# All of layer 1's modulation and both MLP gates: from TensorE to sums on VectorE, GpSimd and ScalarE inside the MLPs

## The chip, the core and the metric

The kernel runs on one core of a Trainium2 chip. The metric is the device time of one execution in microseconds, the median of the runs shown. The engines are named as in the profile: PE is TensorE (PEld its weight loads), DVE is VectorE, ACT is ScalarE, POOL is GpSimd, SP is the engine that issues most DMAs.

## What is computed

One step of a two-layer transformer block on 384 tokens (128 context, 256 latent) of 1024 features. Each layer takes a modulation from a conditioning vector, one vector `m` for the context tokens and one for the latent tokens:

```python
e = silu(m) @ w_ada + b_ada                       # w_ada: 1024 x 6144, per layer
sh1, sc1, g1, sh2, sc2, g2 = split(e, 6)          # 1024 each
h = rmsnorm(x, g_mix) * (1 + sc1) + sh1
x = x + g1 * (mix(h) @ w_out)                     # mix: projection, four head groups
hf = rmsnorm(x, g_ffn) * (1 + sc2) + sh2
x = x + g2 * (square(relu(hf @ w_ff1)) @ w_ff2)   # 1024 -> 4096 -> 1024
```

`mix` is a projection into four groups (neighbourhood attention A, differential attention B, latent attention C, spatial gating D). So `sh1, sc1` are wanted when a layer begins, `g1, sh2, sc2` at its output projection, and `g2` only at the second matrix of its MLP. Everything is float32.

## The kernel before

Activations lie feature by token: a tile is 128 features by 384 tokens, and `x` is eight such tiles. Each large product is made of three float32r products (`mm3`, lines 201 to 203): weights and activations are split into a high part (a cast on ScalarE, L192) and a low part (raw minus high, L193, on VectorE or, where `pool` is set, on GpSimd). `load_split` first calls `load_raw` (L185), which issues a DMA of 512 KB on SP's queue into one of seven raw buffers; high and low parts have four buffers each.

An MLP runs in two halves. Each half makes 16 hidden tiles (24 matmuls each), then eight output tiles with two weight tiles each (48 matmuls). A hidden tile is read out of PSUM by VectorE (L1028, L1029), goes through relu and square on ScalarE (L1031, L1033), is squared in full on GpSimd (L1034), and VectorE takes the low part (L1035). An output tile is added to `x` with its gate by VectorE (`residual`, L852). In the second half of layer 0, `gained` (L363 to L364) and `sq_add` (L340) prepare layer 1's inputs from each output tile, and `load_layer(1)` fetches layer 1's small constants at output tile 0.

The modulation is made in three ways:
- `ada_quarter` (L293): layer 0's `sh1, sc1`, at the start, by TensorE.
- `ada(l, g)` (L228): a third of a layer's modulation (2048 columns) by TensorE, with silu(m) as the 32 stationary columns and raw weights streaming past; 16 raw tiles, 32 matmuls (64 records), then four transposes and an addition of the bias. `ada(l, 1)` gives `g1, sh2` and `ada(l, 2)` gives `sc2, g2`, in both layers. They are generators in a list `todo`, and `fill` advances the first by a step (two raw tiles) between the pieces of attention.
- `ada_rows` (L270): layer 1's `sh1, sc1`, by VectorE in layer 0's MLP. Weights are stored transposed (an output feature per partition), `silu_rows` makes silu of both vectors on every partition (it loads 1 MB into the tile that held the keys of group C), and one instruction multiplies 1024 weights by a vector and sums along the row. A block of 128 features takes one raw tile and two such sums; there are 16 blocks. The products that nobody needs go to a scratch `junk`, which has the one buffer of the small constants, and onto the raw tile.

The attention stage (`attend`) goes through units of a head and a block of tokens; after each it calls `pull`, for the next pieces of projections and output blocks, and `fill`. The fractions FILL_A, FILL_B, FILL_C say how many of both. The framework orders each engine's instructions by program order and expected readiness; an engine then executes in that order and waits at the first instruction that isn't ready. SP's queue is in order too.

Of the kernel before, what the change touches and what calls it, by code (L numbers as in the profile page):

```python
# [13 lines left out]
AF = mybir.ActivationFunctionType  # L14
# [66 lines left out]
def hybrid_step(ctx: ExitStack, tc: tile.TileContext, I, O):  # L81
# [15 lines left out]
    def sb(pool, shape, tag, bufs=None, dt=F32):  # L97
        return pool.tile(shape, dt, name=nm(tag), tag=tag, bufs=bufs)
# [41 lines left out]
    def V(n):  # L140
        a, b = VC[n]
        return vec[:, a:b]
# [105 lines left out]
        E[l, g] = eT  # L248


    def silu_rows():
        t = sb(act, [P, 2 * D], "kC", 1)
        nc.sync.dma_start(t, I["m_rows"])
        for c in range(0, 2 * D, 512):
            u = sb(wk, [P, 512], "pc", 3)
            nc.vector.tensor_scalar_max(u, t[:, c:c + 512], -40.0)
            nc.scalar.activation(u, u, AF.Exp, scale=-1.0)
            nc.scalar.activation(u, u, AF.Ln, bias=1.0)
            nc.scalar.activation(u, u, AF.Exp, scale=-1.0)
            nc.vector.tensor_mul(t[:, c:c + 512], t[:, c:c + 512], u)  # L260
        return t


    def ada_rows(rows, junk):
        eT = sb(lay, [P, 16, 2], "eT0")
        t = sb(lay, [P, 16, 2], "eTs")
        for b in range(16):
            raw = load_raw(I["w_adaT"][b], D)
            for v, out in enumerate((junk[:, 0:D], raw)):
                nc.vector.tensor_tensor_reduce(  # L270
                    out, raw, rows[:, v * D:(v + 1) * D], 1.0, 0.0, ALU.mult, ALU.add, t[:, b, v:v + 1]
                )
            yield
        nc.vector.tensor_add(
            eT, t, V("b_ada1")[:, 0:16].rearrange("p (j o) -> p j o", o=1).to_broadcast([P, 16, 2])
        )
        E[1, 0] = eT

# [285 lines left out]
    for l in range(L):  # L566
# [35 lines left out]
        else:  # L602

            for b in range(6):
# [2 lines left out]
                    mm3(accs[b][:, 0:TX], [t[:, k * P:(k + 1) * P] for t in w], hx1[k], k == 0, k == KD - 1)  # L607
                if b == 0:
                    rstd = x_rstd(acc)
        todo.append(ada(l, 1))  # L610
        todo.append(ada(l, 2))
        kfA = pair()
        nc.gpsimd.dma_start(kfA[:, :, 0:TP], I["kc"][l, 0])

# [391 lines left out]

        complete(work, last)
        e1 = M["e1"] = ada_done(l, 1)
        e2 = ada_done(l, 2)
        M["g2"] = gain(e2[:, 0:8, :], V(f"g_ffn{l}"))  # L1010
        for g in outs:
            for _ in g:
                pass
# [5 lines left out]
        for half in range(2):  # L1019
            hid = []  # L1020
            for m in range(KF // 2):
                w = load_split(I["w_ff1"][l, half * (KF // 2) + m], 1024)
                a = ps_mm()
                for k in range(KD):
                    mm3(a[:, 0:TX], [t[:, k * P:(k + 1) * P] for t in w], hs[k], k == 0, k == KD - 1)
                r = sb(wk, [P, TX], "rl", 2)[:, 0:T]
                bias = sb(wk, [P, 2], "rb", 2)
                nc.vector.tensor_copy(bias, a[:, T:TX])  # L1028
                nc.vector.tensor_mul(r, a[:, 0:T], rstd)  # L1029
                for v, (c, d) in enumerate(((0, TP), (TP, T))):  # L1030
                    nc.scalar.activation(r[:, c:d], r[:, c:d], AF.Relu, bias=bias[:, v:v + 1])  # L1031
                hi, lo = hilo()
                nc.scalar.activation(hi, r, AF.Square)  # L1033
                nc.gpsimd.tensor_mul(r, r, r)  # L1034
                nc.vector.tensor_sub(lo, r, hi.bitcast(F32))  # L1035
                hid.append((hi, lo))
                if l + 1 < L:
                    if half == 0 and m == 3:
                        rows = silu_rows()
                        junk = sb(lay, [P, SMW], "small", 1)  # L1040
                        todo.append(ada_rows(rows, junk))
                    fill(m % 3 == 2)
            for m in range(KD):
                a = ps_mm()
                for q in range(2):
                    w = load_split(I["w_ff2"][l, half, m, q], 1024, q)
                    for i in range(8):
                        k = 8 * q + i
                        mm3(a[:, 0:T], [t[:, i * P:(i + 1) * P] for t in w], hid[k], k == 0, k == 15)
                residual(a, m, e2[:, 8:16, :])  # L1050
                if half == 0:
                    fill()
                else:
                    if l + 1 < L:
                        if m == 0:
                            e0 = ada_done(1, 0)
                            load_layer(1)
                            g1 = gain(e0[:, 8:16, :], V(f"g_mix{l + 1}"))
                            hx1 = []
                        hx1.append(gained(m, g1[:, m, :], e0[:, m, :]))  # L1060
                    if m < KD - 1 or l + 1 < L:
                        sq_add(acc, m)
                    if l + 1 == L and m < 3:

                        if m % 2 == 0:
                            ys.append(pair())
                        nc.scalar.activation(
                            ys[m // 2][:, m % 2, :], x[:, m, :], AF.Copy, scale=V("g_final")[:, m:m + 1]
                        )
# [183 lines left out]
```

## Time and profile before

| | |
|---|---|
| median of 3 runs | 1021.88 us (1017.98 to 1025.13) |
| profiled execution | 1022.66 us, of which the profile's span is 1020.8 |
| mean granted clock of TensorE | 0.987 of 2.4 GHz |
| busy: PE, DVE, ACT, POOL | 966.7, 631.8, 461.6, 269.8 us |
| layer 0's MLP | about 248 to 521 us of the span |
| layer 1's projection and attention | about 521 to 738 |
| layer 1's MLP | about 738 to 1007 |

A row of the profile names the line, the engine, the operation and its tiles (output <- inputs); "idle before" is time in which that engine stood before the instruction, with what ended the wait.

### The profile page before, as it was taken

Reading aid. Unit: us, or ns where it says so; the run is one execution under the profiler, and the core shown is the slowest. Engines: PE = TensorE matmul, PEld = TensorE weight load, DVE = VectorE, ACT = ScalarE, POOL = GpSimd, SP = SyncE. Lnnn points to the kernel's source line nnn. Section 1 sums busy time; section 2 is a strip of 40 time slices with the busy share of each in tenths; the row PEclk is TensorE's granted clock in tenths of the full one; section 3 lists DMA queues with packets and bytes.
Section 4 is the critical chain, followed back from the end, with each engine's and each line's share of the span. In section 5 each row is a group of like instructions: output and inputs, shape, how many; then the busy total and the mean of one; then the engine's idle time right before and its main releaser. Section 6 shows DMA issues by size and latency. Waiting matters only on the chain.

```text
span 1020.8 us, 14701 instructions
## 1 busy us (share of the span) xinstructions
PE 966.7 (95%) x5358; PEld 852.1 (83%) x5358; DVE 631.8 (62%) x1285; ACT 461.6 (45%) x917; POOL 269.8 (26%) x240
## 2 busy tenths in 40 slices
PE   6999899898999999999998979998999999999995
PEld 2687566578998999999997756656999999999994
DVE  4475588879677556646676738886865322554453
ACT  3343576665553224553334427575455422455320
POOL 2353140220224211132243415111021421113221
PEclk9999899999999999999999998999999999999998
DMA  9868585735454555433435475663433334333301
GB/s 360 317 190 261 186 261 179 281 107 158 153 167 143 186 205 182 152 120 122 129 112 198 140 248 176 243 215 120 160 109 125 120 124 139 126 125 109 122 1 62
DMA packets 54744, 169.20 MB, mean 166 GB/s; under 512 B 7856, under 2 KB 11856, under 8 KB 54288
## 3 DMA queue, kind: packets, MB, share of 16 engines
q1 hardware_dynamic: 44928, 152.54, 43.7%
q0 software_dynamic: 6048, 10.94, 3.8%
q10 hardware_dynamic: 3696, 4.79, 1.5%
q8 instruction: 42, 0.69, 0.3%
q14 instruction: 30, 0.25, 0.1%
HBM read 160.19 MB, written 8.03 MB: 165 GB/s over the span
## 4 chain that ended last, share of the span: by engine, by line
PE 55%; DVE 5%; issue 2%; POOL 2%; DMA 2%; ACT 2%; ACTq 1%; DVEq 0%; POOLq 0%
PE mm L202 17%; PE mm L201 17%; PE mm L203 17%; PE ada L228 1%; DMA raw<-in_w_inT 1%; PE t L510 1%; ACT whi L192 1%; PE t L497 1%; DVE pair L198 1%; POOL h L349 1%; DMA pair<-in_bias 1%; ACTq L390 0%; DVE wlo L193 0%; POOL wlo L193 0%; DVE h L351 0%
## 5 line engine op out<-in xcount | busy, mean ns | idle before, releaser
L201 PE MATMUL mm<-pair,whi 128*128 128x384 f32 (+1 forms) x1296 | 443.9, 343 | 9.3 <-ACT pair L197 4.4
L202 PE MATMUL mm<-pair,whi 128*128 128x384 f32 (+1 forms) x1296 | 440.2, 340 | 5.0 <-DVE pair L198 3.7
L203 PE MATMUL mm<-pair,wlo 128*128 128x384 f32 (+1 forms) x1296 | 438.8, 339 | 0.0
L192 ACT CAST whi<-raw 128x1024 fp32r<-128x1024 f32 (+2 forms) x188 | 194.0, 1034 | 341.9 <-PE mm L202 262.8
L201 PEld LDWEIGHTS mm<-pair,whi 128*128 128x128 f32 x1296 | 243.0, 188 | 24.2 <-ACT pair L197 9.4
L202 PEld LDWEIGHTS mm<-pair,whi 128*128 128x128 f32 x1296 | 244.1, 188 | 9.7 <-DVE pair L198 7.0
L203 PEld LDWEIGHTS mm<-pair,wlo 128*128 128x128 f32 x1296 | 245.0, 189 | 3.4 <-issue 3.3
L193 DVE TENSOR_TENSOR wlo<-raw,whi 128x1024 fp32r<-128x1024 f32 (+2 forms) x135 | 162.7, 1205 | 88.9 <-ACT whi L192 88.3
L193 POOL TENSOR_TENSOR wlo<-raw,whi 128x1024 fp32r<-128x1024 f32 (+1 forms) x53 | 128.8, 2431 | 325.7 <-ACT whi L192 310.5
L1034 POOL TENSOR_TENSOR rl<-rl 128x384 f32<-128x384 f32 x64 | 58.3, 912 | 264.9 <-ACT pair L1033 150.8
L1035 DVE TENSOR_TENSOR pair<-rl,pair 128x384 fp32r<-128x384 f32 x64 | 40.1, 626 | 80.8 <-POOL rl L1034 80.8
L852 DVE SCALAR_TENSOR_TENSOR x<-mm,eT,x 128x128 f32<-128x128 f32 x96 | 35.5, 411 | 62.5 <-PE mm L203 62.5
L1031 ACT ACTIVATE rl<-rl,rb 128x128 f32<-128x128 f32 (+1 forms) x128 | 51.1, 446 | 21.1 <-DVE rl L1029 20.9
L228 PE MATMUL ada<-raw,sT 128*32 128x512 f32 x256 | 46.7, 606 | 0.0
L497 PEld LDWEIGHTS t<-ident,pl 128*128 128x128 f32 x144 | 17.0, 140 | 24.7 <-issue 15.4
L1029 DVE TENSOR_TENSOR rl<-mm,xr 128x384 f32<-128x384 f32 x64 | 35.0, 548 | 0.1
L1033 ACT ACTIVATE pair<-rl 128x384 fp32r<-128x384 f32 x64 | 33.6, 525 | 2.0
L480 ACT ACTIVATE pl<-s,nmx 128x384 f32<-128x384 f32 x48 | 28.0, 583 | 13.6 <-DVE nmx L476 13.2
L476 DVE TENSOR_REDUCE nmx<-s 128x1 f32<-128x384 f32 x48 | 26.3, 549 | 10.6 <-PE s L953 6.4
L270 DVE CUSTOM_DVE_ANT_0 small<-raw,kC 128x1024 f32<-128x1024 f32 x16 | 22.6, 1413 | 15.5 <-DMA raw<-in_w_adaT 15.5
L497 PE MATMUL t<-ident,pl 128*128 128x128 f32 x144 | 24.9, 279 | 5.9 <-DVE pl L997 4.5
L498 ACT COPY pair<-t 128x384 f32<-128x384 f32 x48 | 22.5, 478 | 15.9 <-PE t L497 10.2
(261 smaller groups left out, 1096.1 us busy)
## 6 DMA issues: line engine op xcount, KB each, us to landing
raw<-in_w_ff SPq DMA_DIRECT2D x128, 512.0 KB
raw<-in_w_ada SPq DMA_DIRECT2D x64, 512.0 KB
raw<-in_w_inT SPq DMA_DIRECT2D x20, 512.0 KB
adaq<-in_w_ada SPq DMA_DIRECT2D x32, 256.0 KB
raw<-in_w_out SPq DMA_DIRECT2D x16, 512.0 KB
raw<-in_w_adaT SPq DMA_DIRECT2D x16, 512.0 KB
raw<-in_w_inV SPq DMA_DIRECT2D x8, 512.0 KB
raw<-in_w_inV SPq DMA_DIRECT2D x8, 416.0 KB
```

Source lines behind the costliest of these rows:

```text
L192: nc.scalar.copy(hi, raw)
L193: (nc.gpsimd if pool else nc.vector).tensor_sub(lo, raw, hi.bitcast(F32))
L201: nc.tensor.matmul(out, lhsT=l[0], rhs=r[0], start=start, stop=False)
L202: nc.tensor.matmul(out, lhsT=l[0], rhs=r[1], start=False, stop=False)
L203: nc.tensor.matmul(out, lhsT=l[1], rhs=r[0], start=False, stop=stop)
L228: nc.tensor.matmul(acc[32 * j:32 * j + 32, :], lhsT=sT[:, k, :], rhs=raw[j // 2][:, (j % 2) * 512:(j % 2) * 512 + 512], start=(k == 0), st ...
L497: nc.tensor.transpose(tp[:, c * P:(c + 1) * P], p[:, c * P:(c + 1) * P], ident)
L852: nc.vector.scalar_tensor_tensor(x[:, m, a:b], acc_ps[:, a:b], gate[:, m, v:v + 1], x[:, m, a:b], ALU.mult, ALU.add)
L1029: nc.vector.tensor_mul(r, a[:, 0:T], rstd)
L1031: nc.scalar.activation(r[:, c:d], r[:, c:d], AF.Relu, bias=bias[:, v:v + 1])
L1034: nc.gpsimd.tensor_mul(r, r, r)
L1035: nc.vector.tensor_sub(lo, r, hi.bitcast(F32))
```

## The change

`ada` is kept for `ada(0, 1)` alone. A new `ada_half(0)` makes `sc2` of layer 0 in the old way from 1024 columns. All else goes through a class `Rows`, a list of blocks that are made one at a time by `step`: layer 0's `g2` (8 blocks) and all of layer 1's modulation but its `g2` gate (40 blocks) in layer 0's MLP, and layer 1's `g2` (8 blocks) in layer 1's MLP. A block goes to VectorE (two multiply-and-sum instructions, as before) or to GpSimd and ScalarE: GpSimd multiplies (`tensor_mul`, twice), ScalarE passes over the product and sums it. `silu_rows` is called at hidden tile 1 in both layers, and `load_layer(1)` moves from output tile 0 to output tile 7 of the second half.

```diff
+    def ada_half(l):
+        acc = ps_ada()
+        for kk in range(KD // 2):
+            raw = [load_raw(I["w_ada"][l, 2, 2 * kk + i, 0], 1024) for i in range(2)]
+            for i in range(2):
+                for h in range(2):
+                    j = 2 * i + h
+                    nc.tensor.matmul(
+                        acc[32 * j:32 * j + 32, :],
+                        lhsT=sT[:, 2 * kk + i, :],
+                        rhs=raw[i][:, h * 512:h * 512 + 512],
+                        start=(kk == 0), stop=(kk == KD // 2 - 1),
+                    )
+            yield
...
+    class Rows:
...
+        def begin(self):
+            self.rows = silu_rows()
+            self.junk = sb(lay, [P, SMW], "small", 1)
+
+        def add(self, l, name, first, n):
+
+            eT = sb(lay, [P, n, 2], f"eT{name}")
+            for b in range(n):
+                self.items.append((l, name, first, n, b, eT))
+
+        def step(self, vector=0, pool=0):
+            for i in range(vector + pool):
+                if not self.items:
+                    return
+                l, name, first, n, b, eT = self.items.pop(0)
+                raw = load_raw(I["w_adaT"][first + b + (8 if l else -40)], D)
+                for v in range(2):
+                    row = self.rows[:, v * D:(v + 1) * D]
+                    if i < vector:
+                        nc.vector.tensor_tensor_reduce(
+                            raw if v else self.junk[:, 0:D], raw, row, 1.0, 0.0, ALU.mult, ALU.add,
+                            eT[:, b, v:v + 1],
+                        )
+                    else:
+                        to = raw if v else self.junk[:, D:2 * D]
+                        nc.gpsimd.tensor_mul(to, raw, row)
+                        nc.scalar.activation(to, to, AF.Copy, accum_out=eT[:, b, v:v + 1])
+                if b == n - 1:
+                    nc.vector.tensor_add(
+                        eT, eT,
+                        V(f"b_ada{l}")[:, first:first + n].rearrange("p (j o) -> p j o", o=1)
+                        .to_broadcast([P, n, 2]),
+                    )
+                    E[l, name] = eT
...
-        todo.append(ada(l, 1))
-        todo.append(ada(l, 2))
+        if l == 0:
+            todo.append(ada(0, 1))
+            todo.append(ada_half(0))
...
-        e2 = ada_done(l, 2)
-        M["g2"] = gain(e2[:, 0:8, :], V(f"g_ffn{l}"))
+        M["g2"] = gain(ada_done(l, "g"), V(f"g_ffn{l}"))
...
-                if l + 1 < L:
-                    if half == 0 and m == 3:
-                        rows = silu_rows()
-                        junk = sb(lay, [P, SMW], "small", 1)
-                        todo.append(ada_rows(rows, junk))
-                    fill(m % 3 == 2)
+                if half == 0:
+                    if m == 1:
+                        R.begin()
+                        R.add(l, "r", 40, 8)
+                        if l + 1 < L:
+                            R.add(1, 0, 0, 16)
+                            R.add(1, 1, 16, 16)
+                            R.add(1, "g", 32, 8)
+                    elif l + 1 == L:
+                        R.step(vector=3 <= m < 11)
+                    elif m > 2:
+                        R.step(vector=m % 2, pool=m in (4, 10))
+                elif l + 1 < L:
+                    R.step(vector=m % 3 == 0, pool=m % 3 == 1)
...
-                residual(a, m, e2[:, 8:16, :])
+                residual(a, m, E[l, "r"])
                 if half == 0:
-                    fill()
+                    if l + 1 < L:
+                        R.step(vector=2 if m < 6 else 1, pool=m % 2 == 0)
                 else:
                     if l + 1 < L:
+                        R.step(vector=m < 7, pool=m in (0, 2, 4))
+                        if m == KD - 1:
+                            assert not R.items
+                            load_layer(1)
                         if m == 0:
-                            e0 = ada_done(1, 0)
-                            load_layer(1)
+                            e0 = E[1, 0]
```

`ada_rows` is dropped, and the host lays out the transposed weights of 56 blocks instead of 16.

## Rows read from the trace of the kernel before

**Rows 1.** The page: busy us of TensorE, share of the span, instructions
```profile
PE 966.7 (95%) x5358; PEld 852.1 (83%) x5358; DVE 631.8 (62%) x1285; ACT 461.6 (45%) x917; POOL 269.8 (26%) x240
```

**Rows 2.** Busy time by stretch (start:end, length, then busy us of each engine)
```profile
core 0: us, PE busy (x) PEld busy (x) DVE busy (x) ACT busy (x) POOL busy (x), PEclk, DMA share, GB/s
385.30:453.60 68.30, 68.30 (x387) 68.30 (x386) 42.62 (x77) 35.99 (x62) 15.66 (x16) 1.00 0.48 158
453.60:520.90 67.30, 67.30 (x385) 67.30 (x385) 41.65 (x60) 23.99 (x33) 20.62 (x9) 1.00 0.39 123
540.00:617.00 77.00, 65.78 (x329) 50.96 (x328) 45.56 (x106) 31.46 (x79) 26.59 (x31) 0.94 0.59 190
617.00:700.00 83.00, 80.71 (x476) 52.07 (x476) 69.21 (x192) 53.80 (x151) 19.70 (x22) 0.99 0.66 228
...
150.00:200.00 50.00, 47.02 (x276) 28.54 (x275) 41.31 (x102) 32.28 (x83) 6.82 (x4) 1.00 0.65 224
```

**Rows 3.** The same, of the instructions of line 228 alone
```profile
540.00:617.00 77.00, 5.09 (x32) 0.85 (x32) 0.94 0.59 190
617.00:700.00 83.00, 18.25 (x96) 2.59 (x96) 0.99 0.66 228
...
150.00:200.00 50.00, 11.64 (x64) 1.65 (x64) 1.00 0.65 224
```

**Rows 4.** Timeline, TensorE and ScalarE, 606 to 614 (start us, length us; idle before)
```profile
606.99 0.52 PE L497 MATMUL t<-ident,pl 128*128 128x128 f32 x3 [1.12 <-DVE pl L905]
613.08 0.70 PE L506 MATMUL t<-pcT,pair 128*64 128x128 f32 x4 [5.58 <-ACT pair L498]
...
611.60 1.04 ACT L192 CAST whi<-raw 128x1024 fp32r<-128x1024 f32 x1 [3.36 <-DMA raw<-in_w_inT]
```

**Rows 5.** Waits of SP's DMA queue, 585 to 700 and 200 to 522 (total, times, longest)
```profile
SPq L185 <- PE ada L228: 51.1, 12, 9.3
...
SPq L253 <- PE t L497: 7.5, 1, 7.5
```

**Rows 6.** Groups by line: operation, shapes, count; busy us, mean ns; idle before
```profile
L192 ACT CAST whi<-raw 128x1024 fp32r<-128x1024 f32 (+2 forms) x188 | 194.0, 1034 | 341.9 <-PE mm L202 262.8 <-issue 26.2 <-DMA raw<-in_w_inT 23.1
L193 DVE TENSOR_TENSOR wlo<-raw,whi 128x1024 fp32r<-128x1024 f32 (+2 forms) x135 | 162.7, 1205 | 88.9 <-ACT whi L192 88.3 <-PE s L896 0.2
L193 POOL TENSOR_TENSOR wlo<-raw,whi 128x1024 fp32r<-128x1024 f32 (+1 forms) x53 | 128.8, 2431 | 325.7 <-ACT whi L192 310.5 <-DVE wlo L193 15.1
...
L852 DVE SCALAR_TENSOR_TENSOR x<-mm,eT,x 128x128 f32<-128x128 f32 x96 | 35.5, 411 | 62.5 <-PE mm L203 62.5
L1029 DVE TENSOR_TENSOR rl<-mm,xr 128x384 f32<-128x384 f32 x64 | 35.0, 548 | 0.1
```

**Rows 7.** Timeline, VectorE, 326 to 342
```profile
326.94 1.23 DVE L270 CUSTOM_DVE_ANT_0 small<-raw,kC 128x1024 f32<-128x1024 f32 x1
328.09 0.08 DVE L270 DVE_READ_ACCUMULATOR2_ANT eTs<- 128x1 f32 x1
328.21 3.29 DVE L270 CUSTOM_DVE_ANT_0 raw<-raw,kC 128x1024 f32<-128x1024 f32 x1
...
336.22 3.27 DVE L270 CUSTOM_DVE_ANT_0 small<-raw,kC 128x1024 f32<-128x1024 f32 x1 [2.92 <-DMA raw<-in_w_adaT]
...
339.62 1.23 DVE L270 CUSTOM_DVE_ANT_0 raw<-raw,kC 128x1024 f32<-128x1024 f32 x1
```

**Rows 8.** Timeline, GpSimd, 326 to 342
```profile
327.55 2.87 POOL L193 TENSOR_TENSOR wlo<-raw,whi 128x1024 fp32r<-128x1024 f32 x1 [2.26 <-ACT whi L192]
336.00 2.40 POOL L193 TENSOR_TENSOR wlo<-raw,whi 128x1024 fp32r<-128x1024 f32 x1 [5.58 <-ACT whi L192]
```

**Rows 9.** Timeline, SP's queue, 195 to 262 and 480 to 526
```profile
208.50 0.33 SPq L253 DMA_DIRECT2D kC<-in_m_rows  x1
...
482.53 20.10 SPq L185 DMA_DIRECT2D raw<-in_w_inT  x6
```

**Rows 10.** Timeline, VectorE, 205 to 216
```profile
213.36 0.43 DVE L256 TENSOR_SCALAR pc<-kC 128x512 f32<-128x512 f32 x1 [2.44 <-DMA kC<-in_m_rows]
```

More of the change, by code (lines that the diff above doesn't have):

```diff
@@ L248, in ada @@
         E[l, g] = eT
+    def ada_half(l):
[12 more added lines that the diff above has]
+            yield
+        e = sb(wk, [P, 512], "pc", 3)
+        nc.scalar.copy(e, acc)
+        tp = ps_t()
+        for b in range(4):
+            nc.tensor.transpose(tp[:, b * P:(b + 1) * P], e[:, b * P:(b + 1) * P], ident)
+        eT = sb(lay, [P, 8, 2], "eTh")
+        tv = tp.rearrange("p (b i h q) -> p i h b q", b=4, i=2, h=2)[:, :, :, :, 0:2]
+        to = eT.rearrange("p (h b) v -> p h b v", h=2)
+        bias = V(f"b_ada{l}")[:, 32:40]
+        nc.vector.tensor_tensor(
+            to, tv[:, 0], bias.rearrange("p (h b o) -> p h b o", h=2, o=1).to_broadcast([P, 2, 4, 2]), ALU.add,
+        )
+        nc.vector.tensor_tensor(to, tv[:, 1], to, ALU.add)
+        E[l, "g"] = eT
     def silu_rows():
@@ L261, in silu_rows, with __init__ @@
         return t
[L264 to L277, printed above, removed]
+    class Rows:
+        def __init__(self):
+            self.items = []
+            self.rows = None
+        def begin(self):
[27 more added lines that the diff above has]
+                        .to_broadcast([P, n, 2]),
+                    )
+                    E[l, name] = eT
+    R = Rows()
     def load_quarter(q):
@@ L1175 @@
     )
-    in_["w_adaT"] = np.ascontiguousarray(A["w_ada"][1, :, :2 * D].T).reshape(16, P, D)
+    wt = [A["w_ada"][0, :, 5 * D:].T, A["w_ada"][1].T]
+    in_["w_adaT"] = np.ascontiguousarray(np.concatenate(wt)).reshape(56, P, D)
     in_["vec"] = vec
```

## The prediction, made before the changed kernel was run

> **What bounds the kernel now.** I read the page's busy shares first. TensorE works 966.7 of 1020.8 us [rows 1], so time leaves only where TensorE gets shorter or stops waiting. Then busy time by stage [rows 2]: the second half of layer 0's MLP is wholly TensorE: 385.3 to 453.6 is its first matrix, 16 tiles in 68.3 us (4.27 each), and 453.6 to 520.9 its second, 16 tiles in 67.3 us (4.21). Such an MLP takes at least 2 x (68.3 + 67.3) = 271.2 us. In layer 1's attention the picture is another one: 617 to 700 is tight (80.71 of 83), with VectorE close behind (69.21), while 540 to 617 leaves TensorE 11.2 us idle at a granted clock of 0.94. Third, the same stretches for the modulation's line 228 alone [rows 3]: 5.09 and 18.25 us in layer 1, 11.64 us in 150 to 200 (layer 0's second block). Fourth, the waits around the hole at 606 to 613 [rows 4, 5], then the prices [rows 6] and who blocks whom [rows 7, 8].
>
> **What leaves TensorE.** Layer 1 loses both blocks, 5.09 + 18.25 = 23.3 us; layer 0 loses half of its second, 11.64 / 2 = 5.8 us. What that is worth by place:
> - 617 to 700: removing 18.25 us would leave TensorE some 62 of 83, but VectorE's 69.21 stay. So at most 83 - 69.2 = 13.8 us come back. I take 12, since VectorE also waits on chains; ends 0 and 18.
> - 540 to 617: TensorE waits 5.58 us for ScalarE's copy L498, which stands behind a weight cast that itself waited for its DMA [rows 4]. That load was late because SP's queue stood 51.1 us, in 12 waits, for modulation matmuls to release raw buffers [rows 5]. Without those loads the wait should go: 6 us with the 1.12 before it. The granted clock of 0.94 over 77 us [rows 2] is 4.6 us of TensorE's full rate; the low level follows the hole, and I take 3 of it. Of the 5.09 us of matmuls I take 2; the rest stand beside other waits. Sum 11, ends 2 and 16.
> - 150 to 200: 4 of 5.8 us, in the proportion of 12 to 18.
> Together 27 us gained; ends some 2 and 40.
>
> **What comes into layer 0's MLP.** 48 blocks instead of 16: VectorE 7, 14, 6, 7 and GpSimd 2, 4, 5, 3 in the four stretches (first and second matrix of each half). Each block is two passes over 128x1024. One of VectorE is 1.15 us from start to start and 0.12 for its accumulator read [rows 7]. One of GpSimd isn't in the trace; nearest is its subtraction of the same size, 2.43 us [rows 6]. ScalarE's 28 sums, near the cast's 1.03 us, are some 30 us in a stage where that cast mostly waits for TensorE (262.8 us over the kernel, rows 6): no cost while ScalarE isn't held by a late GpSimd.
> By busy time all fits. But the two engines exclude each other. GpSimd starts a subtraction of 2.40 us at 336.00 [rows 8]; the VectorE sum that starts at 336.22 takes 3.27 instead of 1.23 [rows 7], so it began to run at 338.26: GpSimd held it out for 2.27 us. The other way round, GpSimd's at 327.55 takes 2.87 = 2.40 + 0.47 because VectorE's sum of 326.94 ran on to 328.02, a hold of 1.08. So I add holds: 1.08 for a VectorE pass or low part, 2.27 for GpSimd's, and 384/1024 of these (0.41, 0.85) for the hidden tile's two operations and for the passes of 384 at the end.
> - First half, first matrix: 16 x (1.08 + 0.41 + 0.85) + 14 x 1.08 + 4 x 2.27 + 4 x 0.54 (silu, half the columns) = 63.9 us, TensorE 68.3.
> - First half, second matrix: 8 x 1.08 + 28 x 1.08 + (8 + 8) x 2.27 = 75.1, TensorE 67.3.
> - Second half, first matrix: 16 x 2.34 + 12 x 1.08 + 10 x 2.27 = 73.2, TensorE 68.3.
> - Second half, second matrix: 8 x 1.08 + 16 x 0.41 + 14 x 1.08 + (8 + 6) x 2.27 = 62.1, TensorE 67.3.
> Beside that VectorE has work outside the lock: 0.55 a tile for the read of PSUM, 0.41 twice a tile for the residual [rows 6], as much again for the next layer's gains, 0.19 around each sum, 4 x 0.43 for silu: 13.2, 11.9, 11.1 and 15.9, together 52.1 us. Where GpSimd holds the lock this runs for nothing; otherwise it adds. If all is hidden, only two stretches exceed TensorE, by 7.8 + 4.9 = 12.7 us. If none is, all do, by 274.3 + 52.1 - 271.2 = 55.2. I take a third exposed, as GpSimd enters at the moment VectorE's hold ends [rows 8]: 274.3 + 17.4 - 271.2 = 20.5. Against it stands what is split ahead: four weight buffers, three of them ahead of TensorE, 3 x 4.2 = 12.6 us. So the stage costs 8 us more; ends 0 and 43. No gain is possible there, since nothing leaves it.
> The loads move too: 32 more of 512 KB in this MLP on SP's queue, some 60 GB/s on top of 123 to 158 [rows 2]; the row of 540 to 617 moved 190. I cost them at nothing; if raw buffers held by late sums delay weights, it is inside the upper end. The 1 MB load of silu's input moves two tiles up in the same queue, where it stood 7.5 us for attention C to release its tile [rows 5]; the weights of tiles 2 and 3, now behind it, are wanted some 40 us later (it was issued at 208.50, rows 9, and the half of 135.6 us that they belong to ends at 385.3): nothing, or the 7.5 if that lead is gone.
>
> **The rest.** Layer 1's own MLP gets 8 sums on eight consecutive tiles: holds of 1.08 + 0.41 + 0.85 + 2.16 = 4.50 and a third of 0.93, 4.8 against 4.27, so 4.3 us late, under the 12.6 ahead; with its second silu, which now also waits for a 1 MB load, I take 1, ends 0 and 5. At the layers' border the load of the small constants moves from tile 0 to tile 7. It waits for the last sum (tile 6) to release the scratch, and behind it in SP's queue stand layer 1's first weights, which now begin to load at 482.53, some 39 us before use [rows 9]. A 1 MB load of this queue issued at 208.50 was waited for until 213.36 [rows 9, 10], 4.9 us; half of that for the first 512 KB behind it, and 1.03 + 1.21 for cast and low part: 9.6 us after the release, which comes 6 to 7 us before TensorE wants the tile. 3 us, ends 0 and 9.
>
> **The sum**, from the profiled execution's 1022.66 us (0.8 above the median of 1021.88): - 27 + 8 + 1 + 3 = - 15, so 1007.7 us.
>
> **The rivals.** (a) The lock decides. If VectorE's other work isn't hidden, layer 0's MLP is 43 us longer instead of 8: 1042.7, slower. It breaks even when the stage costs 23 more, that is when (23 + 12.6 - 3.1) / 52.1 = 0.62 of that work is exposed. For it: waits of 2.0 us on VectorE already now, with half the work. Against it: no TensorE wait came of these so far (68.30 of 68.30). (b) Attention doesn't shrink from 617 to 700, nor in layer 0, as softmax chains through VectorE and ScalarE set the pace: 11 gained instead of 27, 1023.7. For it: VectorE at 83% there. Against: TensorE at 97%. The Trainium skill, "Perfetto Trace Analysis", Identifying the Most-Contended Engine, says that matmul busy time is a poor measure and weight-load busy time a better one; by that TensorE has 52.07 of 83 us and VectorE is the limit, which is this rival. No run here has yet shown which. (c) The work ahead covers all: nothing lost in layer 0's MLP or at the border, 996.7. For it: the holds alone add up to 274 us, 3 above TensorE's. Against: two stretches exceed it by themselves.
>
> **How the numbers follow.** Forecast 0.43 (its own range 997 to 1020), (a) 0.25, (b) 0.15, (c) 0.17. One per cent, what a measurement here can tell, is 10.2 us. Faster by more: 0.25 of the forecast's and all of (c), 0.42. Within: 0.18, 0.10 of (b) and 0.05 of (a), 0.33. Slower: 0.20 of (a) and 0.05 of (b), 0.25. The range is 992 to 1042: it leaves out the lower part of (c) and the upper half of (a), 2 in 10 together.
>
> **What would show it.** Right: layer 1's attention 20 us or more shorter, without a hole of 5 us before its second group; layer 0's MLP 5 to 20 us longer, with VectorE's sums and low parts stretched to 3 us beside GpSimd's products, and TensorE's waits on low parts, mostly in the second matrix of half 0 and the first of half 1; a wait of a few us for weights at the border. Wrong: that MLP longer by over 25 us, or TensorE idle in layer 1's attention by as much as was removed.

## The result, and the profile after

The changed kernel takes 1085.69 us (median of 4 runs, 1084.47 to 1089.97) and the kernel before 1020.89 beside it: 1.0638 times as long, with a 95% interval of 1.0604 to 1.0671. The forecast was 1007.7, its range ended at 1042, and the dearest rival stood at 1042.7. Everything here compares profiled spans, 1084.1 us now and 1020.8 before.

The page's busy time, to be read beside [rows 1]:

```profile
PE 973.7 (90%) x5190; PEld 874.5 (81%) x5190; DVE 726.4 (67%) x1400; ACT 495.3 (46%) x983; POOL 362.1 (33%) x268
```

TensorE has 168 matmuls fewer and is busy 7 us longer in a span 63 us longer. So it waits, and what it runs takes longer.

Where the time lies is told by marks that both TensorE timelines have: the two matmuls of x_rstd, which stand at the head of each MLP and behind the first tile of layer 1's projection, and the change of the moving operand from 386 to 384 columns between an MLP's matrices. From mark to mark (start of layer 0's MLP, start of layer 1's attention, taken behind that first tile, start of layer 1's MLP, end) the kernel before has 248.1, 277.9, 212.7 and 282.1 us, and the changed one 247.0, 342.0, 207.7 and 287.4. The differences are -1.1, +64.1, -5.0 and +5.3 us and add up to the 63.3 between the spans.

Layer 0's MLP, its four stretches in the changed kernel (half 0: first and second matrix; half 1: the same). Columns: stretch, length, then busy time of TensorE, its weight loads, VectorE, ScalarE and GpSimd, granted clock, DMA share, GB/s:

```profile
246.99:326.86 79.87, 70.29 (x361) 68.00 (x361) 65.15 (x103) 38.60 (x68) 31.17 (x19) 0.94 0.54 177
326.86:414.81 87.95, 74.17 (x385) 71.99 (x385) 64.95 (x75) 28.61 (x42) 50.90 (x19) 0.92 0.57 186
414.81:510.53 95.72, 76.78 (x385) 73.88 (x385) 59.29 (x91) 45.33 (x80) 43.29 (x25) 0.93 0.51 159
510.53:583.97 73.44, 69.54 (x385) 68.46 (x386) 54.92 (x85) 27.36 (x42) 27.79 (x12) 0.98 0.55 174
```

The kernel before, in the half that [rows 2] doesn't show:

```profile
248.13:316.44 68.31, 65.41 (x364) 64.56 (x364) 50.57 (x86) 35.62 (x62) 17.50 (x15) 1.00 0.50 162
316.44:385.33 68.89, 67.78 (x386) 67.33 (x385) 40.96 (x56) 18.43 (x20) 19.42 (x9) 1.00 0.51 177
```

Two readings. TensorE's 385 matmuls of a stretch take 67 to 68 us at full clock and 70 to 77 now: it has to wait, the granted clock of the four stretches is 0.92 to 0.98, and so part of the loss appears as busy time. And no engine is full: in the worst stretch, 95.72 us, VectorE is busy for 59.29 and GpSimd for 43.29. Work that waits in line, not work that doesn't fit, sets that stretch.

The waits of that MLP (247 to 584; engine, what waited, for whom; total us, times, longest):

```profile
...
ACT small L327 <- POOL small L326: 63.9, 12, 11.7
...
POOL small L326 <- DMA raw<-in_w_adaT: 45.9, 11, 11.6
...
DVE pair L1094 <- POOL rl L1093: 38.0, 29, 5.6
...
DVE wlo L193 <- ACT whi L192: 26.5, 13, 7.4
...
PE mm L201 <- DVE rl L1088: 21.6, 10, 3.7
...
PE mm L201 <- DVE x L912: 14.2, 8, 3.6
```

Line 326 is GpSimd's product, 327 ScalarE's sum of it, 1093 GpSimd's square of a hidden tile, 1088 and 912 VectorE's two reads of PSUM. TensorE's own waits are for these reads, which stand in VectorE's queue behind sums and behind whatever VectorE waits for. A long wait alone isn't a loss: for the squares VectorE stood as long in this MLP of the kernel before (248 to 521), where TensorE lost nothing in the second half [rows 2]:

```profile
DVE pair L1035 <- POOL rl L1034: 38.0, 30, 3.6
```

The start of the worst stretch shows the line, engine by engine (start, length, idle before). GpSimd:

```profile
423.83 2.37 POOL L326 TENSOR_TENSOR small<-raw,kC 128x1024 f32<-128x1024 f32 x1 [11.65 <-DMA raw<-in_w_adaT]
...
440.26 2.73 POOL L326 TENSOR_TENSOR small<-raw,kC 128x1024 f32<-128x1024 f32 x1 [1.78 <-DMA raw<-in_w_adaT]
443.07 2.40 POOL L326 TENSOR_TENSOR raw<-raw,kC 128x1024 f32<-128x1024 f32 x1
445.42 0.84 POOL L1093 TENSOR_TENSOR rl<-rl 128x384 f32<-128x384 f32 x1
```

ScalarE:

```profile
426.23 1.06 ACT L327 ACTIVATE small<-small 128x1024 f32<-128x1024 f32 x1 [10.02 <-POOL small L326]
...
429.77 1.03 ACT L192 CAST whi<-raw 128x1024 fp32r<-128x1024 f32 x1
```

VectorE:

```profile
430.84 1.23 DVE L193 TENSOR_TENSOR wlo<-raw,whi 128x1024 fp32r<-128x1024 f32 x1 [7.42 <-ACT whi L192]
...
446.29 0.56 DVE L1094 TENSOR_TENSOR pair<-rl,pair 128x384 fp32r<-128x384 f32 x1 [5.55 <-POOL rl L1093]
```

A product waits 11.65 us for its load, the sum behind it 10.02, the weight cast behind that sum starts at 429.77, and VectorE stands 7.42 us for that cast. Some 15 us later VectorE stands 5.55 us for a square that is queued behind two products.

Layer 1's attention, mark to mark, of the changed kernel:

```profile
589.01:796.68 207.67, 184.30 (x959) 155.05 (x959) 163.22 (x397) 116.47 (x283) 59.34 (x60) 0.95 0.37 114
```

and of the kernel before:

```profile
526.00:738.66 212.66, 197.12 (x1090) 150.54 (x1090) 157.00 (x385) 110.84 (x272) 56.57 (x60) 0.98 0.55 183
```

TensorE's busy time fell by 12.8 us where 23.3 us of matmuls left [rows 3], and the stretch by 5.0. That is no more than this stretch varies by itself: in the eleven runs below that share the changed kernel's attention it takes 203.3 to 212.9 us, and in two that share the attention of before 209.3 and 211.4.

### The profile page after: what moved, and what is told of

Read it like the earlier page. It is cut to its first block, busy times and chain, and to the rows that moved or that the text cites. A ratio compares the mean times of both kernels' runs of the same rounds, so it can differ in the third digit from the quotient of the medians.

```text
span 1084.1 us, 14594 instructions
## 1 busy us (share of the span) xinstructions
PE 973.7 (90%) x5190; PEld 874.5 (81%) x5190; DVE 726.4 (67%) x1400; ACT 495.3 (46%) x983; POOL 362.1 (33%) x268
## 4 chain that ended last, share of the span: by engine, by line
PE 32%; DVE 13%; POOL 8%; issue 7%; DMA 4%; ACT 4%; DVEq 0%; POOLq 0%; ACTq 0%
PE mm L201 10%; PE mm L202 10%; PE mm L203 10%; DMA raw<-in_w_adaT 3%; POOL raw L326 2%; POOL wlo L193 2%; POOL small L326 1%; DVE wlo L193 1%; DVE raw L320 1%; DMA pair<-in_bias 1%; POOL rl L1093 1%; DVE small L320 1%; DVE pair L198 1%; DVE x L912 1%; ACT rl L1090 1%
## 5 line engine op out<-in xcount | busy, mean ns | idle before, releaser
L201 PE MATMUL mm<-pair,whi 128*128 128x384 f32 (+1 forms) x1296 | 456.7, 353 | 60.8 <-DVE rl L1088 25.8
L202 PE MATMUL mm<-pair,whi 128*128 128x384 f32 (+1 forms) x1296 | 451.1, 348 | 2.3 <-DVE pair L1094 1.1
L203 PE MATMUL mm<-pair,wlo 128*128 128x384 f32 (+1 forms) x1296 | 448.4, 346 | 1.6 <-POOL wlo L193 1.6
L201 PEld LDWEIGHTS mm<-pair,whi 128*128 128x128 f32 x1296 | 251.3, 194 | 82.1 <-issue 45.4
L202 PEld LDWEIGHTS mm<-pair,whi 128*128 128x128 f32 x1296 | 252.3, 195 | 6.6 <-DVE pair L198 3.4
L193 POOL TENSOR_TENSOR wlo<-raw,whi 128x1024 fp32r<-128x1024 f32 (+1 forms) x53 | 137.3, 2592 | 278.3 <-ACT whi L192 263.3
L1093 POOL TENSOR_TENSOR rl<-rl 128x384 f32<-128x384 f32 x64 | 64.1, 1002 | 233.2 <-ACT pair L1092 135.1
L320 DVE CUSTOM_DVE_ANT_0 small<-raw,kC 128x1024 f32<-128x1024 f32 x42 | 65.7, 1565 | 14.0 <-DMA raw<-in_w_adaT 13.8
L320 DVE CUSTOM_DVE_ANT_0 raw<-raw,kC 128x1024 f32<-128x1024 f32 x42 | 69.6, 1658 | 1.1 <-DVE eT L320 0.5
L326 POOL TENSOR_TENSOR small<-raw,kC 128x1024 f32<-128x1024 f32 x14 | 39.2, 2800 | 50.4 <-DMA raw<-in_w_adaT 45.9
L912 DVE SCALAR_TENSOR_TENSOR x<-mm,eTr,x 128x128 f32<-128x128 f32 x64 | 23.7, 411 | 44.0 <-PE mm L203 44.0
L327 ACT ACTIVATE small<-small 128x1024 f32<-128x1024 f32 x14 | 14.9, 1061 | 67.7 <-POOL small L326 67.7
L326 POOL TENSOR_TENSOR raw<-raw,kC 128x1024 f32<-128x1024 f32 x14 | 39.2, 2797 | 1.0
```

The lines of the kernel that those rows point to most:

```text
L193: (nc.gpsimd if pool else nc.vector).tensor_sub(lo, raw, hi.bitcast(F32))
L201: nc.tensor.matmul(out, lhsT=l[0], rhs=r[0], start=start, stop=False)
L202: nc.tensor.matmul(out, lhsT=l[0], rhs=r[1], start=False, stop=False)
L203: nc.tensor.matmul(out, lhsT=l[1], rhs=r[0], start=False, stop=stop)
L320: nc.vector.tensor_tensor_reduce(raw if v else self.junk[:, 0:D], raw, row, 1.0, 0.0, ALU.mult, ALU.add, eT[:, b, v:v + 1],)
L326: nc.gpsimd.tensor_mul(to, raw, row)
```

## The experiments

Each run's time stands with its ratio to the kernel before on the same chip, and its interval. "MLP" is the length of layer 0's MLP (its four stretches together: 272.8 us before, 337.0 after; its start is read to within 0.7 us). The expectations of the first three weigh against each other that ScalarE's queue is held by late products (W), that VectorE and GpSimd shut each other out (L), and that VectorE's own work is too much (V).

**All sums by VectorE.** `if i < vector:` becomes `if True:`, so the 14 blocks of GpSimd and ScalarE go to VectorE.

> The changed kernel, with its 14 GpSimd blocks made by VectorE at the same places (48 blocks there, GpSimd and ScalarE none). Theory W (ScalarE's queue is held: its sum waits for GpSimd's product, the product for its load, the load for a raw buffer that ScalarE's late casts should release): nearly all of the 64 us that layer 0's MLP lost comes back, 1025 to 1040 us. Theory L (the lock between VectorE and GpSimd alone): holds fall by 28 x (2.27 - 1.08) = 33 us, 1050 to 1060. Theory V (VectorE has too much): 36 us more of it, 1090 or more.

1047.07 us, 1.0246 [1.0185, 1.0307]; MLP 301.6: between what W and what L had expected. More work for VectorE, and 39 us less than the changed kernel, so V falls. VectorE's load is not the main part, but with 32 blocks more than before in this MLP it costs 25 to 30 us by itself.

**No sums by ScalarE.** `nc.scalar.activation(to, to, AF.Copy, accum_out=...)` is left out, and with it the values of these blocks.

> The changed kernel without ScalarE's 28 sums; GpSimd's products stay, VectorE writes zeros in place of the sums, so these parts of the modulation are left out. Theory W: ScalarE waits for GpSimd no longer, 1025 to 1045 us. Theories L and V: GpSimd and VectorE do what they did, so 1080 to 1086.

1080.78, 1.0576 [1.0512, 1.0639]; MLP 330.6. The intervals overlap with the changed kernel's, so the 10-us waits of ScalarE above are worth some 5 us or nothing: without them nearly all of the delay is still there.

**ScalarE's sums made independent of the products.** They read the silu row, in two pieces, in the place of GpSimd's product.

> As the run without sums, but ScalarE does passes of the same number of columns over the silu row, which is ready (two of 512 columns each for one of 1024, into an idle PSUM bank): ScalarE's work without its wait; these parts of the modulation are left out. Theory W: within 10 us of the run without sums. If ScalarE's load is what costs, not its wait: near 1086.

1081.31, 1.0581 [1.0507, 1.0654], as without any sums. Theory W falls: ScalarE's place in the chain isn't the cause.

**No loads.** `raw = load_raw(...)` becomes `raw = self.rows[:, 0:D]`, once with the changed kernel's engines and once with VectorE alone.

> All 56 blocks with the changed kernel's sums, products and places, but none of the loads of the modulation's weights: each sum and product reads the silu row itself and writes to scratch (the modulation's values are thereby left out). Theory R (the raw buffers and their loads decide: a buffer held by a late sum or product keeps SyncE from issuing the next weights): most of the 65 us comes back, 1020 to 1045 us. Theory L (the lock between GpSimd's products and VectorE's sums) and theory Q (the in-order queues: VectorE waits for GpSimd's squares of the MLP's hidden rows, which stand behind products): loads don't matter, 1070 to 1085 us.

> All sums by VectorE, none by GpSimd or ScalarE, and none of their loads (the sums read the silu row; the modulation's values are thereby left out). Beside the run with all sums by VectorE and its loads (1047 us). Theory R: 1015 to 1030 us. Theories L and Q: GpSimd's part is gone in both, so what is left is VectorE's own queue: 1040 to 1050 us. The difference between this run and the one above is then the price of the products on GpSimd: under L and Q about 35 us, under R less than 15.

1089.45, 1.0645 [1.0554, 1.0736], and 1044.8, 1.0209 [1.014, 1.0278]. Each is as slow as its twin with the loads, but only the second compares like with like. Its four stretches are 77.9, 78.4, 78.3 and 67.0 us beside 77.1, 79.9, 78.0 and 66.9 with the loads. So with VectorE alone the loads, their buffers and their place in SyncE's queue cost nothing that can be seen. In the first run the scheduler, with no load to reckon with, moved the blocks forward. The first stretch:

```profile
255.94:373.80 117.86, 79.71 (x361) 75.58 (x361) 111.33 (x123) 56.86 (x104) 78.19 (x37) 0.85 0.19 63
```

VectorE is full there, and the third and fourth stretches have no block left and take 68.25 and 66.93. That the total came out as before is chance, and what late loads cost beside products is open. The next runs keep every load.

**Fills instead of products.** In the kernel without ScalarE's sums, GpSimd's `tensor_mul(to, raw, row)` becomes two, and in the second run three, `memset(..., 0.0)`.

> The changed kernel without ScalarE's sums (that kernel ran in 1080.8 us), and with each product of GpSimd replaced by two fills of the same tile with zero: GpSimd's queue stays occupied for about as long and the loaded tile is held as before, but no operation of GpSimd reads two tiles beside VectorE (the sums of GpSimd's blocks are left out). Theory L, if a fill doesn't shut VectorE out: 1045 to 1060 us. Theory Q: 1070 to 1085 us as long as a pair of fills lasts about 2.3 us, since the squares of the hidden rows stand behind them as they stood behind the products; in proportion less if the fills are shorter. Theory R: 1070 to 1085 us.

> As the run with fills, but three fills of 0.95 us in the place of each product, 5.7 us for a block: GpSimd's queue is now occupied as long as by the two products (5.4 us), without an operation that reads beside VectorE. The run with two fills in all for a block (the records show 1.9 us for it) took 1041.1 us. Theory Q (the squares of the hidden rows wait behind the products in GpSimd's queue, and VectorE behind the squares): 1070 to 1085 us. Theory L (the lock while both engines run decides, not how long GpSimd is occupied): 1040 to 1052 us.

1041.12, 1.0173 [1.0098, 1.0248], and 1037.16, 1.0156 [1.0124, 1.0189]; MLP 292.7 with the long fills. GpSimd's groups over the kernel, with products and no sums by ScalarE (count; busy us, mean ns; idle before):

```profile
L326 POOL TENSOR_TENSOR small<-raw,kC 128x1024 f32<-128x1024 f32 x14 | 40.6, 2903 | 53.0 <-DMA raw<-in_w_adaT 38.2 <-DVE eT L320 9.7 <-DVE x L913 3.6
L326 POOL TENSOR_TENSOR raw<-raw,kC 128x1024 f32<-128x1024 f32 x14 | 37.2, 2656 | 4.1 <-issue 3.2
```

and with long fills:

```profile
L326 POOL MEMSET raw<- 128x1024 f32 x84 | 80.5, 959 | 50.1 <-DMA raw<-in_w_adaT 12.5 <-issue 10.0 <-DVE eT L320 9.7
```

GpSimd is occupied for 77.8 us by the one and 80.5 by the other, and the kernel is 44 us shorter with the fills. (The first run's fills take 54.4 us, 3.9 for a block; the 1.9 in the expectation of the second is wrong.) What counts is not how long GpSimd is busy, but what it does meanwhile.

Single instructions show it. A product in the changed kernel, and the sum that VectorE starts beside it:

```profile
331.86 2.60 POOL L326 TENSOR_TENSOR raw<-raw,kC 128x1024 f32<-128x1024 f32 x1
332.12 3.43 DVE L320 CUSTOM_DVE_ANT_0 small<-raw,kC 128x1024 f32<-128x1024 f32 x1
```

Fills, and a sum beside them (the run with long fills and no squares, below):

```profile
396.10 6.02 POOL L326 MEMSET raw<- 128x1024 f32 x6 [5.15 <-DMA raw<-in_w_adaT]
400.95 1.23 DVE L320 CUSTOM_DVE_ANT_0 small<-raw,kC 128x1024 f32<-128x1024 f32 x1 [0.77 <-DMA raw<-in_w_adaT]
```

In layer 0's MLP the sums that overlap with nothing on GpSimd take 1.21 to 1.23 us. So do all 18 that overlap with fills alone, in the two runs with long fills. Six that overlap with products alone, in the changed kernel, take 2.59 in the mean and up to 3.42.

**Copies instead of products.** `tensor_mul` becomes two `tensor_copy` of a tile.

> The changed kernel without ScalarE's sums, and with each product of GpSimd replaced by a plain copy of a tile of the same size: one operand read instead of two (the sums of GpSimd's blocks are left out). With products 1080.8 us, with fills that last as long as the products 1037.2. If any operation of GpSimd that reads a tile takes turns with VectorE's operations on two tiles: well above the fills, 1055 to 1080 us by the copies' length. If only two operands do it: 1035 to 1045 us.

1063.38, 1.0405 [1.0353, 1.0456]. The copies take 77.5 us in all. For the same time of GpSimd: nothing read, 1037; one tile read, 1063; two tiles read, 1081.

**No squares.** The order of GpSimd's queue is the scheduler's choice, and it had put squares between the fills but behind pairs of products. So GpSimd's `tensor_mul(r, r, r)` was left out of layer 0's MLP, with products, with long fills, and with all sums on VectorE.

> The changed kernel without ScalarE's sums (1080.8 us), and in layer 0's MLP also without GpSimd's squaring of the hidden rows (left out of the computation): VectorE's low part of the hidden row then waits for ScalarE alone. Theory Q (VectorE stands behind GpSimd's products, since it needs the square that is queued behind them): 1035 to 1050 us, near the run with fills and no squares. Theory L (while a product runs, VectorE's operations on two tiles are shut out, wherever they are queued): 1062 to 1080 us.

> The run with long fills in the place of products (1037.2 us), without the squares in layer 0's MLP. Both theories: 1025 to 1037 us. Its distance to the run with products and no squares is the price of the lock alone: under 12 us by Q, over 25 us by L.

> All sums by VectorE (1047.1 us), without the squares in layer 0's MLP. If what VectorE's blocks cost is its stand of 1.3 us in each tile until the square is there (theory Q for VectorE): 1022 to 1034 us. If it is the sums' own time beside VectorE's other work, with the splits that wait behind them: 1040 to 1047 us.

1073.49, 1.0487 [1.0433, 1.0541]; 1027.49, 1.0058 [1.0039, 1.0077]; 1038.32, 1.0143 [1.0097, 1.019], the last between its two expectations. The MLP's four stretches with products:

```profile
250.27:328.45 78.18, 69.32 (x360) 67.21 (x359) 65.44 (x105) 34.56 (x61) 15.49 (x6) 0.94 0.56 185
328.45:412.09 83.64, 72.96 (x386) 71.22 (x385) 54.72 (x70) 18.03 (x19) 44.70 (x17) 0.94 0.57 191
412.09:502.63 90.54, 75.53 (x386) 73.52 (x386) 68.93 (x94) 35.85 (x61) 31.00 (x11) 0.91 0.52 177
502.63:572.22 69.59, 67.68 (x385) 66.83 (x385) 50.63 (x81) 24.10 (x34) 27.64 (x10) 1.00 0.51 170
```

with fills:

```profile
244.60:313.83 69.23, 66.45 (x361) 65.86 (x360) 58.02 (x102) 34.02 (x59) 14.02 (x13) 0.96 0.61 199
313.83:387.80 73.97, 68.97 (x385) 68.12 (x385) 56.53 (x74) 18.99 (x22) 42.69 (x34) 0.98 0.66 221
387.80:457.58 69.78, 68.50 (x386) 68.20 (x385) 53.05 (x91) 36.12 (x61) 33.04 (x34) 1.00 0.64 217
457.58:524.51 66.93, 66.93 (x386) 66.93 (x385) 48.44 (x83) 24.36 (x34) 27.06 (x16) 1.00 0.58 194
```

With no square to wait for, 46 us still lie between products and fills. In the two executions shown it is 50.7 (the one with fills is the fastest of eight), 42.0 of them in this MLP (322.0 against 279.9). Theory L stands: VectorE has 350 instructions there in either and is busy for 239.7 us with the products and 216.0 with the fills, 23.7 more, of which 15.9 lie in the third stretch. VectorE also waits longer for its loads beside products. Its waits for them in this MLP, with products and with fills:

```profile
DVE small L320 <- DMA raw<-in_w_adaT: 59.7, 21, 8.7
DVE small L320 <- DMA raw<-in_w_adaT: 37.0, 19, 5.4
```

The squares, their own time on GpSimd and the waits for them together, are worth 7 us with products (1080.8 to 1073.5), 9 with VectorE alone (1047.1 to 1038.3) and 10 with long fills (1037.2 to 1027.5); only for the last are the intervals well apart.

The Trainium skill, "SBUF — State Buffer", Who interferes with whom, says that a VectorE instruction with two inputs in SBUF contends with a GpSimd instruction that reads SBUF, and not with one that only writes. The three kinds of GpSimd work agree with it (1037, 1063 and 1081 us), and so do the single sums above (1.23 us beside a fill, 3.43 beside a product).

**The 16 blocks of before, moved.** `fill(m % 3 == 2)` becomes `fill(half == 0 and m > 3)`: 12 blocks in the first stretch. Or it goes, and the second stretch gets `fill(2)`: all 16 there in the program's order.

> The kernel before with its 16 blocks of sums only moved: 12 in the first-matrix stretch of the first half, one for every tile from the fifth on, and four in the second-matrix stretch; nothing is added. Theory of busy time: VectorE has 16 times 2.3 us of its own work there and 12 times 2.5 us of sums, 67 us beside 68.3 of TensorE, and the later stretches get emptier: 1020 to 1026 us. Theory Q (VectorE is in order and stands about 1.3 us in each tile until GpSimd has the square, so a tile takes 2.3 + 1.3 + 2.5 = 6.1 us against TensorE's 4.27): 12 times 1.9 us more, 1036 to 1048 us.

> The kernel before with its 16 blocks of sums moved the other way: all in the second-matrix stretch of the first half, two for each of its 8 tiles (5.1 us of sums in 8.6 us of TensorE). Theory Q: nothing in that stretch has VectorE wait for GpSimd, so there is room: 1017 to 1023 us. If instead the number of sums in a stretch decides, wherever it lies: 1028 us or more.

1028.58, 1.0072 [1.0052, 1.0093], and 1023.6, 1.0029 [1.0007, 1.0052]. The first run's first stretch takes 75.7 us in place of 68.3, the second run's second stretch 73.8 in place of 68.9. Both theories had the size of the first wrong: 7 us, against 0 to 5 and 15 to 27. Whether the place matters isn't shown, as the scheduler puts VectorE's sums elsewhere than the program does. By the traces the first run has 26 of its 32 sums in the first stretch, where the kernel before has 12, and the second run has 11 in the first and 21 in the second, where the kernel before has 12 and 14. So it is 7.4 us for 14 sums more and 4.9 for 7 more.

**Layer 1's modulation taken out of the attention, nothing put into the MLP.** In the kernel before, `todo.append(ada(l, 1))` and `ada(l, 2)` for layer 0 alone (layer 1 uses layer 0's values, so its modulation is not computed):

> The kernel before, with layer 1's two TensorE blocks of the modulation left out (layer 0's are used again, so layer 1's modulation beyond its first third is left out): the gain in attention alone. By the prediction's prices layer 1's attention is 23 us shorter, 998 us; by what the changed kernel's trace shows (5 to 9 us shorter there) 1012 to 1016.

1013.94, 0.9928 [0.99, 0.9955]. So the change could bring some 7 us in that attention, 5 to 10 by the interval. Its stretch, as above:

```profile
524.38:727.29 202.91, 182.70 (x955) 153.01 (x954) 157.44 (x382) 110.09 (x270) 56.37 (x60) 0.95 0.33 109
```

Of the 23.3 us of matmuls, 9.8 shorten the stretch; idle time of TensorE grows by 4.7 (15.5 to 20.2); and 8.9 remain as busy time. Some 6 of these are the remaining matmuls, which take longer (176.7 to 182.7 us, by the time that TensorE is busy with other lines than 228) at a clock of 0.95 in place of 0.98; the rest is overlap of line 228's records with others. In its slowest part the clock is 0.79:

```profile
612.00:652.00 40.00, 33.99 (x149) 26.35 (x148) 33.08 (x100) 25.21 (x77) 12.20 (x17) 0.79 0.35 109
```

**The same with less for VectorE, and before with less for VectorE.** The scalings of the softmax weights, `nc.vector.tensor_scalar_mul(p, p, sm)` and its like, run for layer 0 alone.

> The kernel before without layer 1's ada(1, 1) and ada(1, 2) on TensorE (that kernel ran in 1013.9 us), and in layer 1's attention also without the scaling of 24 tiles of weights by the reciprocal of their sums on VectorE (some 13 us of VectorE's time; these parts of the computation are left out). Theory V (once TensorE is emptied, VectorE and the chain of softmax steps through it set the attention's pace): 1003 to 1010 us. Theory P (TensorE with its loads of weights still sets it): 1012 to 1015 us.

> The kernel before with layer 1's modulation on TensorE as it was, and only the same 24 scalings of VectorE left out of layer 1's attention. Theory V: TensorE is full here and sets the pace, so 1017 to 1022 us. Theory P: no difference either, 1018 to 1022 us. If VectorE set the pace already before the change, the same 4 to 10 us come off as in the run beside it: 1011 to 1017 us.

1005.49, 0.9851 [0.9792, 0.9909], and 1021.52, 1.0001 [0.9977, 1.0026]. With TensorE emptied, the 24 scalings left out are 13 us less on VectorE (157.4 to 144.5) and shorten the attention by 8.4 us (202.9 to 194.5; the kernel 1013.9 to 1005.5, with intervals that just touch). With TensorE full, the same 24 are 9 us less on VectorE (157.0 to 147.8) and shorten it by 1.9 (212.7 to 210.8), within its spread, and the kernel by nothing. By this pair TensorE was the limit, by so little that the change would hand it to VectorE at once.

**A smaller change.** Layer 1's ada(1, 2) as 16 more blocks on VectorE, 4, 10, 5 and 13 in the program's four stretches; the rest as before.

> Layer 1's two MLP rows of modulation, ada(1, 2), as 16 more blocks of sums by VectorE, and nothing by GpSimd or ScalarE; ada(1, 1) and layer 0 stay on TensorE as in the kernel before. The 32 blocks stand 4, 10, 5 and 13 in the four stretches of layer 0's MLP. Half of what the kernel without ada(1, 1) and ada(1, 2) gained is 3.7 us, and the stretches of the second matrix took 10 blocks for nothing and 16 for 5 us. So 1015 to 1021 us beside 1020 to 1022, if room in VectorE's queue is what matters; 1026 us or more if any sum beyond before's 16 costs what it costs in the changed kernel (about 1.6 us for each block).

1031.55, 1.0094 [1.0055, 1.0132]. In the execution profiled, one of the longer ones (1036.61), the scheduler has spread the sums evenly, 16, 14, 17 and 15; the stretches take 70.8, 67.4, 72.3 and 71.4 us, and the attention takes 216.1 instead of 212.7, at a clock of 0.94, though half of line 228's matmuls are gone. No kernel tried here that computes the whole beats the one before. Why the attention got longer with less in it was not tried further.

## Why the prediction was wrong, step by step

**Layer 0's MLP: 8 us forecast, 64 measured.** This is the step that failed, and the prediction's own sign of it, this MLP longer by over 25 us, came. The mechanism was named, the two engines' holds were taken from the right rows [rows 7, 8] (2.27 us is GpSimd's hold from its start at 336.00; the sum itself stood 2.04), and the holds were then added in two kinds: those of the lock, and VectorE's 52.1 us of other work, of which "a third" was taken as exposed and 12.6 us of split weights stood against it. With all of the other work exposed, the same sums give 77.1, 87.0, 84.3 and 78.0 us for the four stretches; measured were 79.9, 88.0, 95.7 and 73.4. In all that is 326.4 against 337.0, as if nothing had been hidden and the weights that were ahead had given nothing back. The match by stretches is in part chance: VectorE started 4 of its sums before this MLP and 19, 23, 14 and 8 in the stretches, where the forecast has 14, 28, 12 and 14. "By busy time all fits" was true and told nothing: busy shares of 59.29 and 43.29 us go with a stretch of 95.72.

What the sum lacked is the third stretch's 11 us. There VectorE stood 24.0 us for squares in all, 7.3 more than in the same stretch before, and 7.42 once for a cast held by a sum of ScalarE. That these make up the 11 isn't shown: without the sums and the squares that stretch still takes 90.54. "ScalarE's 28 sums ... no cost while ScalarE isn't held by a late GpSimd" had its condition right, and the condition was broken (63.9 us of waits). But by the run without these sums the price is some 5 us, between 1085.7 and 1080.8, or nothing.

What the runs show in place of it: 40 more blocks all on VectorE (8 of them in layer 1's MLP) cost 33 us (1013.9 to 1047.1); giving 14 of these to GpSimd, meant as relief, costs 34 more (1080.8); the sums on ScalarE some 5. That GpSimd's reading is the cause of the 34 is shown by the fills, with which they are gone (1037.2). How much of the 34 is time in which VectorE is shut out, and how much the lines and late loads that follow, is open, since the scheduler orders each kernel's queue anew; without squares the first was 23.7 of 42.0 between products and fills.

**The attention: 23 us forecast in layer 1, 5.0 measured.** "617 to 700: ... I take 12" and "540 to 617: ... sum 11" both failed. Rival (b) had the cause: VectorE and the softmax steps set the pace, which the pair of runs without scalings shows. It put the gain of both layers at 11; 6.1 came, and the spread of the stretch doesn't tell 11 from 6. The Trainium skill, "Perfetto Trace Analysis", Identifying the Most-Contended Engine, cited there, by whose measure VectorE was the limit, is borne out once TensorE is emptied and not before: the kernel before didn't gain from 24 scalings less on VectorE. "I take 3 of it", the clock's return, didn't come: where 540 to 617 with its 0.94 was, 603 to 680 now has 0.93, and over the whole attention the clock fell from 0.98 to 0.95. TensorE's longest wait there, for the copy that was line 498 and is 557 now, was to go and is 3.7 us instead of 5.58 [rows 4]:

```profile
PE t L569 <- ACT pair L557: 3.7, 1, 3.7
```

Against the run with nothing put into the MLP, 4.8 us more are lost in the changed kernel's attention. That too lies within the spread, and no run shows its cause. At its end, where the second silu and the first sums were placed, VectorE is full, though TensorE still works 33.98 of 37 us:

```profile
760.00:797.00 37.00, 33.98 (x188) 31.61 (x188) 35.40 (x76) 22.63 (x38) 7.51 (x2) 1.00 0.39 122
```

**Layer 0's attention: 4 us forecast, 1.1 measured,** not to be told apart: the mark at its end lies between 243.5 and 255.9 us in the kernels above, most of which share that part.

**Layer 1's MLP: 1 us forecast, 5.3 measured,** just beyond the upper end given (5).

**The border: 3 us forecast, none measured.** The first tile of layer 1 takes 5.04 us, 5.06 before.

**The loads, at nothing: right as far as is known.** With VectorE alone their absence is worth 2 us, inside the intervals; beside products no run here settles it.

**The rivals.** (a) was the right one and too cheap. Its 1042.7 had layer 0's MLP at 43, 21 below the measurement; the attention's gain at 27, 21 above; layer 1's MLP 4 below and the border 3 above: together the 43 us that are missing. It also kept the gains of the forecast, as each rival varied one term, and here two went wrong together. Its "Against it: no TensorE wait came of these so far" was an argument from a third of the blocks.

## What to carry to other kernels

An engine's idle share says nothing of how much more it can take where it stands in a chain with others: add up, stretch by stretch, its work, its waits and the holds of the engine that it excludes, and take as hidden only what a row shows to be hidden. Work on GpSimd that reads tiles, beside a VectorE that reads two, was no relief: here a block moved from VectorE to GpSimd cost 34 / 14 = 2.4 us, nearly as much as VectorE needs for a whole one (2 x 1.27). And before TensorE is emptied in a stage, look at the next engine's busy time there, and at the granted clock afterwards: of 23.3 us of matmuls taken away some 6 came back in that way.

## What the runs showed of the hardware that was not expected

GpSimd's fills of a 128x1024 tile take 0.96 us and cost VectorE nothing that can be seen: no sum beside fills alone took over 1.23 us, and 84 fills, 80.5 us, went with a kernel 10 us faster than the one that gave these blocks to VectorE. Copies of that tile took 1.32 and 1.45 us in the mean, products 2.66 and 2.90.

The granted clock can be part of the price of a wait. In the run without ScalarE's sums a matmul waits 2.59 us, and those that follow soon take 0.53 us instead of 0.34 (timeline, TensorE):

```profile
439.11 0.41 PE L201 MATMUL mm<-pair,whi 128*128 128x386 f32 x1 [2.59 <-DVE rl L1089]
...
440.82 0.53 PE L203 MATMUL mm<-pair,wlo 128*128 128x386 f32 x1
...
443.92 0.34 PE L201 MATMUL mm<-pair,whi 128*128 128x386 f32 x1
```

That is the step from the level of 2.4 GHz to that of 1.2 and back: the granted clock is 1.00 from 436.00 to 439.00, 0.52 from 440.60 to 443.90, and 1.00 again from 443.90 to 446.00. So the 385 matmuls of a stretch were busy for 68.3 us at a clock of 1.00 [rows 2] and for 76.78 at a mean of 0.93 (half 1, first matrix). Not every wait has this price: in the run with less in layer 1's attention, TensorE was idle for 5.8 us of the first 47.6 (524.38 to 572.00), at a clock of 1.00.
